# A delta-rule mixer on one core: the scales of the 16x16 solve by a transpose and one on-chip DMA, and the solve moved behind q's convolution

## The chip, the core and the metric

The kernel runs on one core of a Trainium2 chip. Times are microseconds of device time for one execution. The kernel before took 3308.4, 3311.98 and 3314.25 us in three timed runs; the middle one, 3311.98, is the time before. One more execution was profiled, and all rows are from that one. PE is TensorE, DVE is VectorE, ACT is ScalarE, POOL is GpSimd and SP is SyncE, which issues most of the DMAs.

## What is computed

The reference is one step of a decoder trunk of two layers for 1024 new prompt tokens and 64 sample tokens (8 sequences of 8). Layer 0 mixes tokens with a gated delta rule in 8 heads of 128 columns, layer 1 with HGRN2, and a convolutional feed-forward block follows each. The part that the change touches is the delta rule of one head, in chunks:

```
kb = kc * bc[..., None]
A = jnp.where(strict, jnp.einsum('nbhik,nbhjk->nbhij', kb, kc) * decay, 0.0)
rhs = jnp.concatenate([vc * bc[..., None], kb * jnp.exp(G)[..., None]], axis=-1)
sol = lax.linalg.triangular_solve(A + eye, rhs, left_side=True, lower=True, unit_diagonal=True)
def step(S, xs):
    u = uv_ - jnp.einsum('bhck,bhkv->bhcv', w_, S)
    o = jnp.einsum('bhck,bhkv->bhcv', qg_, S) + jnp.einsum('bhij,bhjv->bhiv', attn_, u)
    S = S * gl_[..., None, None] + jnp.einsum('bhck,bhcv->bhkv', kd_, u)
```

q, k and v come from a projection, a causal convolution of width 4 and a silu; q and k are normalised. The outputs of all heads go through a norm, a gate and the output projection.

## The kernel before

Dense fp32 products are made of three products in a shorter fp32 form: each operand is split into a high and a low part, and `dense` (L109 to L115) adds high by high, high by low and low by high. A weight tile is loaded by SP and split by ACT (L106) and DVE (L107). In the rows, `pp` are the projections of the heads, `po` and `pf` the output projection, and `adap` products of the conditioning that are spread over the heads; DVE adds those up in `adasb` (L184).

One head is a generator, `gdn_head(h)`. The main loop takes turns between two heads, so that the front of head h+1 (projections, decay, solve) stands beside the recurrence of head h. It resumes a generator at each `yield`. Within what the loop gives, the order of instructions on each engine is set by the framework's scheduler, from the program's order, its own cost model and the buffers that are free. Each engine runs its list in order: what stands behind a waiting instruction waits as well.

The steps of a head, in the order of the program: k is projected and convolved. The decay `dec` is made. `Z` is k by k times the decay (L794 to L804), stored to `zd` in DRAM. k is transposed, its norms give `rk`, and three DVE operations give `c1`, `nE` and `c2` (L826 to L828; in the rows these are `gc`). `nE` holds the scale of each token, 128 partitions by 9 columns. The solve wants it with one row of 16 tokens for each of 72 blocks (9 chunks of 8), which is the tile `Ep`, 72 by 16: POOL stores `nE` element by element to `ed` in DRAM (L829) and loads it back (L841). The diagonal blocks of Z come as `Zp` from `zd` (L838). Then q is projected and convolved, `pqk` (k by q, L846 to L855) is made, and q is transposed for its norm (`pq`).

Behind a yield stands the 16x16 solve: `Lp` is `Zp` times `Ep` (L868), and 15 steps of one product (L873) and one reduction (L875) on DVE invert the 72 lower triangles at once, followed by a copy (L876). All are in the tile `fs`. The inverse is stored to `td` (L878), loaded as `mg` (L879) so that four blocks of a chunk lie in their partitions, and ACT masks it (L889, L890). Then v and the gate g are projected. The merge follows: from 16x16 blocks to 32, 64 and 128, in products `pV` (L928, L952, L970), `pT` (L933, L958) and `pX` (L937, L961, L973) on PE, with DVE and ACT between. The first `pV` needs `mg`.

The recurrence goes over 8 chunks: `pKS` (k by S, L994), `ru` (DVE, L996), `pU` (L998), the copy `u` (ACT, L1000), `pS` (L1002), and the new state `sn` (DVE, L1011); `po` (L1005, L1006) collects the output. The sample tokens (L1019 on) and the norm and gate end the head; its output is transposed on PE (`pot`, L650), and POOL stores it to DRAM (`ohl`, L660 and L661). The output projection behind the last head loads these as `og` (L470).

PSUM tiles are of three kinds; transposes, `pqk`, merge products and the output `po` of a head share the three buffers of the kind `mx`.

Of the kernel before, what the change touches and what calls it, by code (L numbers as in the profile page):

```python
# [9 lines left out]
F32 = mybir.dt.float32  # L10
# [4 lines left out]
ALU = mybir.AluOpType  # L15
# [4 lines left out]
NT = 1024  # L20
NS = 64
NTOK = NT + NS
# [4 lines left out]
EPS = 1e-6  # L27
# [15 lines left out]
def trunk_kernel(ctx: ExitStack, tc: tile.TileContext, a: dict, o: dict):  # L43
    nc = tc.nc
# [4 lines left out]
    drp = ctx.enter_context(tc.tile_pool(name="drp", bufs=1, space=DRAM))  # L49

    def big(tag, shape=(128, NTOK), dt=F32, name=None, bufs=None):
        return main.tile(list(shape), dt, tag=tag, name=name or tag, bufs=bufs or {"xp": 2, "wraw": 3, "whl": 3}.get(tag, 1))

    def small(tag, shape, dt=F32, bufs=1, name=None):
        return sm.tile(list(shape), dt, tag=tag, name=name or tag, bufs=bufs)

    def ps(tag, name=None):
        return psp.tile([128, 512], F32, tag=tag, name=name or tag, bufs={"mm": 3, "mx": 3, "rc": 2}[tag])

    mm = nc.tensor.matmul  # L60


    def cload(name, shape, dt=F32):
        t = const.tile(list(shape), dt, name="c_" + name)
        nc.scalar.dma_start(out=t, in_=a[name])
        return t

    ident = cload("ident", [128, 128])
# [96 lines left out]
    def ada_row(l, i, k, tag, ptag, held):  # L165


        w = big(tag, [128, 1024], name="adaw")
        nc.sync.dma_start(out=w, in_=a["ada_w"][l, k * 128:(k + 1) * 128, i * 1024:(i + 1) * 1024])
        if held and k:  # L170
            pt = ada_acc[0]
        else:
            pt = ps(ptag, name="adap")
            ada_turn(None if held else pt)
        for q in range(4):
            mm(pt[32 * q:32 * q + 32, :256], cs[:, k, :], w[:, 256 * q:256 * q + 256], start=(not held or k == 0),
               stop=(not held or k == 7), tile_position=(0, 32 * q))
        if held:
            ada_acc[:] = [pt]
        if k == 0 and not held:  # L180
            ada_acc[:] = [small("adasb", [128, 256], bufs=1)]
            nc.scalar.activation(ada_acc[0], pt[:, :256], AF.Copy)
        elif not held:
            nc.vector.tensor_tensor(ada_acc[0], ada_acc[0], pt[:, :256], op=ALU.add)  # L184
        elif k == 7:
            ada_acc[:] = [small("adasb", [128, 256], bufs=1)]
            nc.scalar.activation(ada_acc[0], pt[:, :256], AF.Copy)
        if k == 7:
            ada_done.append((l, i, ada_acc.pop()))

    def ada_turn(pt=None):

        if not ada_done:
            return
        l, i, sb = ada_done.pop(0)
        p2 = (pt or ps("mx", name="adap2"))[:, 256:512]
        for j in range(2):
            nc.tensor.transpose(p2[:, 128 * j:128 * j + 128], sb[:, 128 * j:128 * j + 128], ident)
        nc.vector.tensor_tensor(
            mods[l][:, 8 * i:8 * i + 8, :].rearrange("p (q j) r -> p j q r", j=2),  # L200
            p2.rearrange("p (j q r) -> p j q r", q=4, r=32)[:, :, :, 0:9],
            adab[:, l, 8 * i:8 * i + 8].rearrange("p (q j) -> p j q", j=2).unsqueeze(3).to_broadcast([128, 2, 4, 9]), op=ALU.add)
# [198 lines left out]
    for g in GORD:  # L401
        hgs[g] = new_hg(g, f"h0{g}")
        t0, n = GRP[g][0], GP[g]
# [9 lines left out]
    for j in range(4):  # L413
# [6 lines left out]
        for g in GORD:  # L420
            t0, n = GRP[g][0], GP[g]
            sc, sh = mod(0, 1), mod(0, 0)
            pt = big("D10", [128, 2, 512], name="pnt")
            for m in range(2 * j, 2 * j + 2):
                t = pt[:, m % 2, :n]
                h = hgs[g][:, 0, m, :n]
# [317 lines left out]
    def ada_step():  # L744
        if rest:
            ada_row(*rest.pop(0), "D10", "mm", False)
        else:
            ada_turn()

    def gdn_head(h):  # L750
        par = h % 2
# [3 lines left out]
        def project(kind, dst):  # L755
            w = load_w(a["w_gin"][h, kind], 1024, "wi")
            return conv_silu(proj(w, hgs, "pp"), kind, h, dst)

        def transposes(src, name, each, evac):

            for b in range(3):
                p = ps("mx", name=name)
                for j in range(4 if b < 2 else 1):
                    t = 4 * b + j
                    n = 128 if t < 8 else 64
                    nc.tensor.transpose(p[:n, 128 * j:128 * j + 128], src[:, 128 * t:128 * t + n], ident)
                for j in range(4 if each and b < 2 else 1 if each else 0):
                    t = 4 * b + j
                    n = 128 if t < 8 else 64
                    each(p[:n, 128 * j:128 * j + 128], t, n)  # L770
                if evac:
                    evac(b, p)

        def sumsq(ss):
            def add(pj, t, n):
                jk = small("junk", [128, 128], bufs=1)
                nc.scalar.activation(jk[:n], pj, AF.Square, accum_out=ss[:n, t:t + 1])
            return add


        k = A(1, "k")
# [3 lines left out]
        dec = big("D2" if par else "D0", name="dec")  # L785
# [27 lines left out]
        def evac_k(b, p):  # L813
# [3 lines left out]
            else:  # L817
# [7 lines left out]
        c1, c2, nE = [small(f"gc{i}", [128, 9], bufs=2) for i in range(3)]  # L825
        nc.vector.scalar_tensor_tensor(c1, rk, 0.5, col(beta), op0=ALU.mult, op1=ALU.mult)  # L826
        nc.vector.scalar_tensor_tensor(nE, c1, -2.0, rk, op0=ALU.mult, op1=ALU.mult)
        nc.vector.tensor_tensor(c2, nE, col(eG), op=ALU.mult)  # L828
        nc.gpsimd.dma_start(out=ed[par].rearrange("(t k) i -> (k i) t", k=8), in_=nE)  # L829


        fs = big("D9", [128, 1024], name="fs")
# [4 lines left out]
        Ep = small("Ep", [72, 16])  # L837
        nc.gpsimd.dma_start(  # L838
            out=Zp, in_=zd[par].rearrange("t x -> (t x)").rearrange("(b y) -> b y", y=2064)[:, :2048].rearrange(
                "b (j i) -> b j i", i=128)[:, :, 0:16])  # L840
        nc.gpsimd.dma_start(out=Ep, in_=ed[par])  # L841
        yield

        q = A(0, "q")
        project(0, q)
        for b in range(3):  # L846
            pq = ps("mx", name="pqk")
            if b < 2:
                for j in range(4):
                    t0 = 512 * b + 128 * j  # L850
                    mm(pq[:, 128 * j:128 * j + 128], k[:, t0:t0 + 128], q[:, t0:t0 + 128], start=True, stop=True)
                nc.vector.tensor_tensor(dec[:, 512 * b:512 * b + 512], pq, dec[:, 512 * b:512 * b + 512], op=ALU.mult)
            else:
                mm(pq[:64, :64], k[:, NT:], q[:, NT:], start=True, stop=True)
                nc.vector.tensor_tensor(dec[:64, NT:], pq[:64, :64], dec[:64, NT:], op=ALU.mult)  # L855
        ada_step()
        qe = small("gqe", [128, 9], bufs=2)
        nc.vector.memset(qe[:, 8:9], 1.0)
        transposes(q, "pq", sumsq(qe), None)
        nc.vector.tensor_scalar(qe, qe, 128 * EPS, 512 * EPS * EPS, op0=ALU.mult, op1=ALU.add)  # L860
        eg = big("D0" if par else "D2", name="eg")
        nc.sync.dma_start(out=eg, in_=gd[1, h:h + 1, :].to_broadcast([128, NTOK]))
        nc.vector.tensor_tensor(q, q, eg, op=ALU.mult)
        qg = q

        yield

        tc.keep_in_program_order(nc.vector.tensor_tensor(Lp, Zp.rearrange("p j i -> p i j"), Ep.unsqueeze(2).to_broadcast([72, 16, 16]), op=ALU.mult))  # L868
        nc.gpsimd.memset(Tp, 0.0)
# [1 line left out]
        for i in range(1, 16):  # L871
# [8 lines left out]
                            in_=td[par].rearrange("(t k) (r x) -> (k r) t x", k=8, x=32))  # L880
# [7 lines left out]
        for e in range(2):  # L888
            nc.scalar.activation(XTc[:, :, :, e, :], cp[:, 0:8], AF.Copy, scale=m16e[:, e:e + 1])  # L889
            nc.scalar.activation(Xs[:, 16 * e:16 * e + 16], cp[:64, 8, 0, :], AF.Copy, scale=m16e[:64, e:e + 1])  # L890

        yield

# [147 lines left out]
        finish(0, h, ot, ot_s, so, qe, gnorm[:, 0:1], gt, ohl0, "D5")  # L1041

    heads = [gdn_head(h) for h in range(H)]

    def stage(h, n=1):
        for _ in range(n):
            if h < H:
                next(heads[h], None)
# [8 lines left out]
    for g in GORD:  # L1057
        p = ps("rc", name="pab")
        t0, n = GRP[g]
# [64 lines left out]
    for b in range(3):  # L1124
        pr = ps("mx", name="pgr")
        ts = [4 * b + j for j in range(4)] if b < 2 else [8]
        for j, t in enumerate(ts):
# [5 lines left out]
    gd = drp.tile([2, 8, NTOK], F32, name="gd")  # L1133
# [2 lines left out]


    zd = drp.tile([2, 9, 16512], F32, name="zd")
    ed = drp.tile([2, 72, 16], F32, name="ed")
    td = drp.tile([2, 72, 512], F32, name="td")  # L1140
    zero = big("D7", [128, 64], name="zero")
    nc.vector.memset(zero, 0.0)
# [1 line left out]
                        in_=zero[64:, :].unsqueeze(1).to_broadcast([64, 2, 64]))  # L1144
# [2 lines left out]
    ohl0 = [drp.tile([128, 2, NTOK], F32, name=f"ohl0{h}") for h in range(H)]  # L1147

    for h in range(H):
        stage(h, 3 if h else 4)  # L1150
        stage(h + 1)
        stage(h)
        stage(h + 1)
        stage(h, 2)
# [360 lines left out]
```

## Time and profile before

| what | value |
|---|---|
| median of three timed runs | 3311.98 us |
| profiled execution, its own time | 3303.52 us |
| its span | 3301.7 us |
| PE busy | 3172.5 us, 96% |
| DVE busy | 1672.8 us, 51% |
| ACT busy | 1101.9 us, 33% |
| POOL busy | 287.6 us, 9% |
| chain that ended last, by engine | PE 86%, DVE 7%, DMA 3%, ACT 2%, issue 2%, POOL 1% |
| the eight heads of layer 0 | about 60 to 840 us of the span |

Busy time is a sum over the whole span; in the heads' stretch the engines share the work differently from the feed-forward blocks. PEclk in a row of stretches is the granted clock of PE as a share of the full 2.4 GHz; 0.50 is the lower level, 1.2 GHz, and a value between is a mean over both. A wait is time in which an engine stood at the head of its list, put down to what released it last.

### The profile page before, as it was taken

How to read it: one execution, taken by the hardware profiler on the slowest of the kernel's cores; microseconds unless marked ns; L12 is line 12 of the kernel's file. 1: busy time of each engine (PE TensorE's matmuls, PEld its weight loads, DVE VectorE, ACT ScalarE, POOL GpSimd, SP SyncE). 2: the span in 40 equal slices, each digit the busy share in tenths (PEclk: the TensorE clock that was granted, in tenths of full speed). 3: DMA queues.
4: the chain of work that ended last, by engine and by line, in shares of the span. 5: the costliest groups of instructions: out<-in, count | busy, mean ns of one | idle time of the engine just before them, and what ended most of it. 6: DMA issues, size and time to landing. Idle time of an engine off the chain costs nothing.

```text
span 3301.7 us, 61857 instructions
## 1 busy us (share of the span) xinstructions
PE 3172.5 (96%) x25449; PEld 2948.0 (89%) x25449; DVE 1672.8 (51%) x3819; ACT 1101.9 (33%) x2611; POOL 287.6 (9%) x639
## 2 busy tenths in 40 slices
PE   7899999998999999999998999999998999999997
PEld 5888888887889999999996999999888999999997
DVE  6677777774562333333447645555465233333345
ACT  5344444442342313131234332333343331222222
POOL 0111111110100000000001000000010000000002
PEclk9999999998999999999998999999999999999999
DMA  6333333234312222222223111112531111111113
GB/s 205 96 105 99 100 100 99 77 93 151 118 61 87 84 83 86 84 87 81 92 63 113 57 62 59 60 63 83 189 104 46 46 46 46 44 44 46 41 63 106
DMA packets 164635, 277.98 MB, mean 84 GB/s; under 512 B 20056, under 2 KB 91480, under 8 KB 164352
## 3 DMA queue, kind: packets, MB, share of 16 engines
q1 hardware_dynamic: 145328, 236.24, 22.7%
q0 software_dynamic: 15616, 37.15, 3.8%
q8 instruction: 200, 3.28, 0.4%
q10 hardware_dynamic: 3408, 0.63, 0.1%
q14 instruction: 83, 0.68, 0.1%
HBM read 222.48 MB, written 51.47 MB: 83 GB/s over the span
## 4 chain that ended last, share of the span: by engine, by line
PE 86%; DVE 7%; DMA 3%; ACT 2%; issue 2%; POOL 1%; ACTq 0%; SPq 0%; POOLq 0%; DVEq 0%
PE pp L113 6%; PE pp L114 6%; PE pp L115 6%; PE pg L113 5%; PE pu L113 5%; PE pg L114 5%; PE pg L115 5%; PE pu L115 5%; PE pu L114 5%; PE pd L113 5%; PE pd L115 5%; PE pd L114 5%; PE pf L113 2%; PE pf L114 1%; PE pf L115 1%
## 5 line engine op out<-in xcount | busy, mean ns | idle before, releaser
L113 PE MATMUL pp<-h,wi 128*128 128x384 f32 (+1 forms) x1536 | 518.8, 339 | 11.9 <-DVE adasb L184 8.5
L115 PE MATMUL pp<-h,wi 128*128 128x384 f32 (+1 forms) x1536 | 518.3, 338 | 0.0
L114 PE MATMUL pp<-h,wi 128*128 128x384 f32 (+1 forms) x1536 | 515.8, 336 | 0.2 <-DVE h L305 0.2
L113 PE MATMUL pg<-h,wg 128*128 128x384 f32 (+1 forms) x1056 | 346.6, 329 | 0.0
L113 PE MATMUL pu<-h,wu 128*128 128x384 f32 (+1 forms) x1056 | 346.3, 328 | 0.0
L115 PE MATMUL pg<-h,wg 128*128 128x384 f32 (+1 forms) x1056 | 346.0, 328 | 0.0
L114 PE MATMUL pg<-h,wg 128*128 128x384 f32 (+1 forms) x1056 | 345.4, 327 | 0.4 <-DVE h L305 0.4
L115 PE MATMUL pu<-h,wu 128*128 128x384 f32 (+1 forms) x1056 | 344.8, 327 | 0.0
L114 PE MATMUL pu<-h,wu 128*128 128x384 f32 (+1 forms) x1056 | 344.3, 326 | 0.0
L113 PEld LDWEIGHTS pp<-h,wi 128*128 128x128 f32 x1536 | 292.4, 191 | 28.2 <-issue 9.0
L113 PE MATMUL pd<-mh,wd 128*128 128x384 f32 (+1 forms) x912 | 299.6, 330 | 0.0
L114 PEld LDWEIGHTS pp<-h,wi 128*128 128x128 f32 x1536 | 292.8, 191 | 6.0 <-DVE wi L107 1.2
L115 PEld LDWEIGHTS pp<-h,wi 128*128 128x128 f32 x1536 | 292.3, 190 | 6.6 <-issue 4.8
L115 PE MATMUL pd<-mh,wd 128*128 128x384 f32 (+1 forms) x912 | 297.4, 326 | 0.0
L114 PE MATMUL pd<-ml,wd 128*128 128x384 f32 (+1 forms) x912 | 297.1, 326 | 0.0
L113 PEld LDWEIGHTS pu<-h,wu 128*128 128x128 f32 x1056 | 198.2, 188 | 7.8 <-issue 6.2
L113 PEld LDWEIGHTS pg<-h,wg 128*128 128x128 f32 x1056 | 199.0, 189 | 6.8 <-issue 6.2
L114 PEld LDWEIGHTS pg<-h,wg 128*128 128x128 f32 x1056 | 199.0, 189 | 1.9 <-issue 1.2
L598 DVE TENSOR_TENSOR facc<-facc,pd 128x384 f32<-128x384 f32 (+1 forms) x192 | 97.6, 510 | 203.1 <-PE pd L115 203.1
L115 PEld LDWEIGHTS pg<-h,wg 128*128 128x128 f32 x1056 | 199.1, 189 | 0.0
L115 PEld LDWEIGHTS pu<-h,wu 128*128 128x128 f32 x1056 | 198.2, 188 | 0.0
L114 PEld LDWEIGHTS pu<-h,wu 128*128 128x128 f32 x1056 | 198.2, 188 | 0.0
(449 smaller groups left out, 5730.9 us busy)
## 6 DMA issues: line engine op xcount, KB each, us to landing
adaw<-in_ada_w SPq DMA_DIRECT2D x96, 512.0 KB, 3.8
wgr<-in_w_gu SPq DMA_DIRECT2D x88, 256.0 KB, 2.7
wur<-in_w_gu SPq DMA_DIRECT2D x88, 256.0 KB, 2.6
wir<-in_w_gin SPq DMA_DIRECT2D x64, 256.0 KB, 2.8
wdr<-in_w_dn SPq DMA_DIRECT2D x64, 256.0 KB, 2.6
wir<-in_w_hin SPq DMA_DIRECT2D x64, 256.0 KB, 2.7
og<-ohl SPq DMA_DIRECT2D x32, 384.0 KB, 7.5
xg<-xd SPq DMA_DIRECT2D x24, 384.0 KB, 4.8
```

The costliest lines, as they stand in the source:

```text
L113: mm(out, wh, rh(k), start=(first and i == 0), stop=False)
L114: mm(out, wh, rl(k), start=False, stop=False)
L115: mm(out, wl, rh(k), start=False, stop=(last and i == len(ks) - 1))
L598: nc.vector.tensor_tensor(am, am, p[:, :n], op=ALU.add)
```

## The change

The way of the scales is changed. PE transposes `nE` into a PSUM tile `pE` of 9 by 128 (kind `mx`), ACT copies it into a part of `fs` (`nEt`), and one DMA issued by SP carries it from there to `Ep`, on chip. The DRAM tile `ed` and the two POOL DMAs go.

The solve, its two DMAs and the two ACT masks move up: they stand directly behind q's projection and convolution, ahead of `pqk`, `pq` and the decay factor of q. One yield goes with that, and the main loop takes one step fewer in a head's first stage. The lines of the solve in the kernel after are L850 (`Lp`), L855, L857 and L858; the merge, recurrence and output lines are two more than before.

```diff
--- before.py
+++ after.py
@@ -826,7 +826,8 @@
         nc.vector.scalar_tensor_tensor(c1, rk, 0.5, col(beta), op0=ALU.mult, op1=ALU.mult)
         nc.vector.scalar_tensor_tensor(nE, c1, -2.0, rk, op0=ALU.mult, op1=ALU.mult)
         nc.vector.tensor_tensor(c2, nE, col(eG), op=ALU.mult)
-        nc.gpsimd.dma_start(out=ed[par].rearrange("(t k) i -> (k i) t", k=8), in_=nE)
+        pe = ps("mx", name="pE")
+        nc.tensor.transpose(pe[:9, :128], nE, ident)
 
 
         fs = big("D9", [128, 1024], name="fs")
@@ -838,11 +839,38 @@
         nc.gpsimd.dma_start(
             out=Zp, in_=zd[par].rearrange("t x -> (t x)").rearrange("(b y) -> b y", y=2064)[:, :2048].rearrange(
                 "b (j i) -> b j i", i=128)[:, :, 0:16])
-        nc.gpsimd.dma_start(out=Ep, in_=ed[par])
+        nEt = fs[:9, 256:384]
+        nc.scalar.copy(nEt, pe[:9, :128])
+        nc.sync.dma_start(out=Ep, in_=nEt)
         yield
 
         q = A(0, "q")
         project(0, q)
+
+        tc.keep_in_program_order(nc.vector.tensor_tensor(Lp, Zp.rearrange("p j i -> p i j"), Ep.unsqueeze(2).to_broadcast([72, 16, 16]), op=ALU.mult))
+        nc.gpsimd.memset(Tp, 0.0)
+        nc.gpsimd.memset(fs[:72, 512 + 16:1024:33], 1.0)
+        for i in range(1, 16):
+            pri = fs[:72, 0:i * i].rearrange("p (c j) -> p c j", j=i)
+            nc.vector.tensor_tensor(pri, Tp[:, 0:i, 0:i].rearrange("p j c -> p c j"),
+                                    Lp[:, i:i + 1, 0:i].to_broadcast([72, i, i]), op=ALU.mult)
+            nc.vector.tensor_reduce(Tp[:, i, 0:i], pri, axis=mybir.AxisListType.X, op=ALU.add)
+        nc.vector.tensor_copy(Xp, Tp.rearrange("p i c -> p c i"))
+        mg = big("D7", name="mg")
+        nc.gpsimd.dma_start(out=td[par], in_=fs[:72, 512:1024])
+        nc.gpsimd.dma_start(out=mg[:, 0:288].rearrange("p (t x) -> p t x", x=32),
+                            in_=td[par].rearrange("(t k) (r x) -> (k r) t x", k=8, x=32))
+
+        cp = mg[:, 0:288].rearrange("p (t i c) -> p t i c", i=2, c=16)
+        XTc = mg[:, 288:800].rearrange("p (t i e c) -> p t i e c", i=2, e=2, c=16)
+        Xs = mg[:64, 800:832]
+        x32 = mg[:, 288:800].rearrange("p (t i c) -> p t i c", i=2, c=32)
+        Xc, Tc = x32[:, :, 0, :], x32[:, :, 1, :]
+        EM, V = [mg[:, i:i + 256].rearrange("p (t c) -> p t c", c=32) for i in (0, 832)]
+        for e in range(2):
+            nc.scalar.activation(XTc[:, :, :, e, :], cp[:, 0:8], AF.Copy, scale=m16e[:, e:e + 1])
+            nc.scalar.activation(Xs[:, 16 * e:16 * e + 16], cp[:64, 8, 0, :], AF.Copy, scale=m16e[:64, e:e + 1])
+
         for b in range(3):
             pq = ps("mx", name="pqk")
             if b < 2:
@@ -862,32 +890,6 @@
         nc.sync.dma_start(out=eg, in_=gd[1, h:h + 1, :].to_broadcast([128, NTOK]))
         nc.vector.tensor_tensor(q, q, eg, op=ALU.mult)
         qg = q
-
-        yield
-
-        tc.keep_in_program_order(nc.vector.tensor_tensor(Lp, Zp.rearrange("p j i -> p i j"), Ep.unsqueeze(2).to_broadcast([72, 16, 16]), op=ALU.mult))
...
-            nc.scalar.activation(Xs[:, 16 * e:16 * e + 16], cp[:64, 8, 0, :], AF.Copy, scale=m16e[:64, e:e + 1])
 
         yield
 
@@ -1136,7 +1138,6 @@
 
 
     zd = drp.tile([2, 9, 16512], F32, name="zd")
-    ed = drp.tile([2, 72, 16], F32, name="ed")
     td = drp.tile([2, 72, 512], F32, name="td")
     zero = big("D7", [128, 64], name="zero")
     nc.vector.memset(zero, 0.0)
@@ -1147,7 +1148,7 @@
     ohl0 = [drp.tile([128, 2, NTOK], F32, name=f"ohl0{h}") for h in range(H)]
 
     for h in range(H):
-        stage(h, 3 if h else 4)
+        stage(h, 2 if h else 3)
         stage(h + 1)
         stage(h)
         stage(h + 1)
```

The order of the engines' lists moves in three places that matter below.

DVE, where the solve of head 4 begins. Before, it stands behind k by q of head 4 (`dec`, `q`) and beside v's convolution:

```order
L855 TENSOR_TENSOR dec<-pqk,dec 64x64
L732 SCALAR_TENSOR_TENSOR v<-gxp,c_gcw,v 128x1024
L863 TENSOR_TENSOR q<-q,eg 128x1088
L868 TENSOR_TENSOR fs<-fs,Ep 72x256
L739 SCALAR_TENSOR_TENSOR v<-gxp,v 128x1088
L860 TENSOR_SCALAR gqe<-gqe 128x9
L873 TENSOR_TENSOR fs<-fs 72x1
L107 TENSOR_TENSOR wi<-wir,wi 128x512
L875 TENSOR_REDUCE fs<-fs 72x1
```

After, it stands inside the recurrence of head 3, whose `ru` and `sn` are L998 and L1013:

```order
L1013 SCALAR_TENSOR_TENSOR sn<-sn,eGL,pS 128x128
L739 SCALAR_TENSOR_TENSOR q<-gxp,q 128x1088
L998 SCALAR_TENSOR_TENSOR ru<-pKS,gc_2907,vb 128x128
L850 TENSOR_TENSOR fs<-fs,Ep 72x256
L184 TENSOR_TENSOR adasb<-adasb,adap 128x256
L855 TENSOR_TENSOR fs<-fs 72x1
L107 TENSOR_TENSOR wi<-wir,wi 128x512
L1013 SCALAR_TENSOR_TENSOR sn<-sn,eGL,pS 128x128
L857 TENSOR_REDUCE fs<-fs 72x1
L855 TENSOR_TENSOR fs<-fs 72x4
L857 TENSOR_REDUCE fs<-fs 72x2
L855 TENSOR_TENSOR fs<-fs 72x9
```

The solve's first steps moved ahead of the end of head 3's recurrence, between the operations on which that recurrence's products wait.

PE, in the middle of head 3's recurrence. Before, one step reads:

```order
L998 MATMUL pU<-ru,X_911 128x128
L115 MATMUL pp<-h_266,wi 128x384
L113 MATMUL pp<-h_266,wi 128x384
L114 MATMUL pp<-h_266,wi 128x384
L1002 MATMUL pS<-ru,kd 128x128
L1006 MATMUL po_5014<-ru,dec 128x128
L115 MATMUL pp<-h_266,wi 128x384
L113 MATMUL pp<-h_266,wi 128x384
L994 MATMUL pKS<-sn,k 128x128
L1005 MATMUL po_5014<-sn,q 128x128
```

After, the step in which `pE` of head 4 comes:

```order
L114 MATMUL pp<-h_266,wi 128x384
L115 MATMUL pp<-h_266,wi 128x384
L830 MATMUL pE<-c_ident,gc_5006 9x128
L1008 MATMUL po_5023<-ru,dec 128x128
L1007 MATMUL po_5023<-sn,q 128x128
L1008 MATMUL po_5023<-ru,dec 128x128
L1007 MATMUL po_5023<-sn,q 128x128
L1004 MATMUL pS<-ru,kd 128x128
L1008 MATMUL po_5023<-ru,dec 128x128
L176 MATMUL adap<-adaw,cs 32x256
L996 MATMUL pKS<-sn,k 128x128
L1007 MATMUL po_5023<-sn,q 128x128
```

The transpose stands ahead of three steps' `po` products and of `pS` of its own step; the next step's `pKS` follows without a dense product between.

PE, around the first merge product `pV` of head 7, the last head. Before, it comes among the output projection's `po` products:

```order
L114 MATMUL po<-og_9114,wo 128x320
L115 MATMUL po<-og_9114,wo 128x320
L113 MATMUL po<-og_9114,wo 128x320
L928 MATMUL pV<-mg,Z 32x32 x32
L114 MATMUL po<-og_9114,wo 128x320
L115 MATMUL po<-og_9114,wo 128x320
L113 MATMUL po<-og_9114,wo 128x320
L114 MATMUL po<-og_9114,wo 128x320
L115 MATMUL po<-og_9114,wo 128x320
L933 MATMUL pT<-mg 32x32 x32
L937 MATMUL pX<-mg 32x32 x32
L952 MATMUL pV<-fs,Z 32x32 x16
```

After, it follows the last `pp` products directly, and `po` begins behind it:

```order
L115 MATMUL pp<-h_266,wi 128x384
L113 MATMUL pp<-h_266,wi 128x384
L114 MATMUL pp<-h_266,wi 128x384
L115 MATMUL pp<-h_266,wi 128x384
L930 MATMUL pV<-mg,Z 32x32 x32
L113 MATMUL po<-og_9127,wo 128x384
L114 MATMUL po<-og_9127,wo 128x384
L115 MATMUL po<-og_9127,wo 128x384
L113 MATMUL po<-og_9127,wo 128x384
L935 MATMUL pT<-mg 32x32 x32
L939 MATMUL pX<-mg 32x32 x32
L954 MATMUL pV<-fs,Z 32x32 x16
```

`pV`, `pT` and `pX` of the last head moved ahead of the first `po`. In the list before, 124 dense products stand between the `pot` of head 6 and this `pV`; in the list after, 28.

## Rows read from the trace of the kernel before

**Rows 1.** Stretches, one row each: length, busy per engine, PEclk, DMA share, GB/s.

```profile
206.00:292.00 86.00, 82.84 (x852) 72.43 (x850) 63.22 (x156) 38.34 (x127) 15.64 (x32) 1.00 0.38 102
```

**Rows 2.** Waits of PE, 140 to 740: total us, times, longest us.

```profile
PE pV L928 <- ACT mg L889: 13.7, 7, 2.9
PE pp L113 <- DVE adasb L184: 8.5, 1, 8.5
```

**Rows 3.** Chain of waits, 404 to 420: start us, us, what.

```profile
409.12 2.82 DMA td<-fs
...
416.69 0.75 PE pV L928 x50
```

**Rows 4.** Chain of waits, 140 to 166, head 0.

```profile
131.27 10.07 DMA ed<-gc
...
141.63 3.81 DMA Ep<-ed
...
156.53 2.24 DMA td<-fs
...
163.36 0.75 PE pV L928 x50
```

**Rows 5.** Waits of PE, 738 to 830, from head 7 on.

```profile
PE pV L928 <- ACT mg L889: 5.7, 1, 5.7
PE po L113 <- DMA og<-ohl: 3.6, 4, 2.1
```

**Rows 6.** Stretches of head 7, after the last projection.

```profile
740.00:758.00 18.00, 14.19 (x67) 12.17 (x67) 8.56 (x26) 2.36 (x5) 1.92 (x3) 0.91 1.03 356
758.00:764.00 6.00, 0.50 (x36) 0.50 (x40) 0.43 (x1) 1.66 (x5) 0.00 (x0) 0.85 0.61 207
764.00:782.00 18.00, 17.82 (x345) 15.71 (x336) 6.56 (x15) 5.33 (x14) 0.00 (x0) 0.86 0.10 31
782.00:790.00 8.00, 6.48 (x38) 4.43 (x40) 2.91 (x7) 2.84 (x11) 0.00 (x0) 0.79 0.11 35
790.00:800.00 10.00, 7.06 (x55) 4.95 (x56) 4.43 (x9) 2.45 (x8) 0.00 (x0) 0.99 0.18 59
800.00:812.00 12.00, 12.00 (x59) 9.12 (x59) 7.41 (x24) 3.72 (x17) 1.49 (x2) 0.58 0.49 154
```

**Rows 7.** Groups of PE, 140 to 830: transposes of a head's output.

```profile
L650 PE MATMUL pot<-c_ident,ot 128*128 128x128 f32 x64 | 8.6, 278 | 2.4 <-DVE ot L645 2.4
```

**Rows 8.** Groups of ACT, 140 to 830: copies of u.

```profile
L1000 ACT COPY ru<-pU 128x128 f32<-128x128 f32 x64 | 16.8, 263 | 68.5 <-PE pU L998 61.2 <-PE pp L115 4.0 <-issue 3.0
```

**Rows 9.** Stretches behind a wait for pV or for head 0's pp.

```profile
156.00:160.00 4.00, 3.49 (x11) 3.49 (x12) 3.96 (x6) 0.00 (x0) 2.04 (x3) 0.50 0.28 82
160.00:164.00 4.00, 3.00 (x74) 2.68 (x72) 1.20 (x2) 1.80 (x5) 0.41 (x2) 0.81 0.19 60
...
412.00:424.00 12.00, 10.24 (x265) 8.57 (x263) 7.10 (x12) 4.98 (x12) 2.06 (x4) 0.86 0.27 82
584.00:596.00 12.00, 10.03 (x266) 8.85 (x265) 7.02 (x13) 5.10 (x12) 2.06 (x4) 1.00 0.16 49
```

**Rows 10.** Groups of DVE, the solve: out<-in, xcount | busy us, mean ns | idle before.

```profile
L873 DVE TENSOR_TENSOR fs<-fs 72x1 f32<-72x1 f32 (+14 forms) x120 | 38.0, 317 | 2.4
...
L875 DVE TENSOR_REDUCE fs<-fs 72x1 f32<-72x1 f32 (+14 forms) x120 | 27.8, 232 | 2.6
```

**Rows 11.** Order of time, DVE, head 3's recurrence: start us, us, line, [idle before].

```profile
355.31 0.17 DVE L827 SCALAR_TENSOR_TENSOR gc<-gc,grk 128x9 f32<-128x9 f32 x1
...
365.59 0.35 DVE L996 SCALAR_TENSOR_TENSOR ru<-pKS,gc,vb 128x128 f32<-128x128 f32 x1 [1.70 <-PE pp L114]
...
372.61 0.35 DVE L996 SCALAR_TENSOR_TENSOR ru<-pKS,gc,vb 128x128 f32<-128x128 f32 x1 [0.58 <-PE pKS L994]
374.44 0.35 DVE L1011 SCALAR_TENSOR_TENSOR sn<-sn,eGL,pS 128x128 f32<-128x128 f32 x1 [1.48 <-PE pS L1002]
```

**Rows 12.** Order of time, POOL, 336 to 372, head 4.

```profile
366.22 0.58 POOL L841 DMA_DIRECT2D Ep<-ed  x1 [9.40 <-DMA ed<-gc]
```

More of the change, by code (lines that the diff above doesn't have):

```diff
@@ L845, in gdn_head @@
         project(0, q)
[L846 to L864, printed above, removed]
-        yield
         tc.keep_in_program_order(nc.vector.tensor_tensor(Lp, Zp.rearrange("p j i -> p i j"), Ep.unsqueeze(2).to_broadcast([72, 16, 16]), op=ALU.mult))
@@ L890, in gdn_head @@
             nc.scalar.activation(Xs[:, 16 * e:16 * e + 16], cp[:64, 8, 0, :], AF.Copy, scale=m16e[:64, e:e + 1])
+        for b in range(3):
+            pq = ps("mx", name="pqk")
+            if b < 2:
+                for j in range(4):
+                    t0 = 512 * b + 128 * j
+                    mm(pq[:, 128 * j:128 * j + 128], k[:, t0:t0 + 128], q[:, t0:t0 + 128], start=True, stop=True)
+                nc.vector.tensor_tensor(dec[:, 512 * b:512 * b + 512], pq, dec[:, 512 * b:512 * b + 512], op=ALU.mult)
+            else:
+                mm(pq[:64, :64], k[:, NT:], q[:, NT:], start=True, stop=True)
+                nc.vector.tensor_tensor(dec[:64, NT:], pq[:64, :64], dec[:64, NT:], op=ALU.mult)
+        ada_step()
+        qe = small("gqe", [128, 9], bufs=2)
+        nc.vector.memset(qe[:, 8:9], 1.0)
+        transposes(q, "pq", sumsq(qe), None)
+        nc.vector.tensor_scalar(qe, qe, 128 * EPS, 512 * EPS * EPS, op0=ALU.mult, op1=ALU.add)
+        eg = big("D0" if par else "D2", name="eg")
+        nc.sync.dma_start(out=eg, in_=gd[1, h:h + 1, :].to_broadcast([128, NTOK]))
+        nc.vector.tensor_tensor(q, q, eg, op=ALU.mult)
+        qg = q
         yield
```

## Prediction

> **What bounds the kernel now.** I first read the engines' busy time on the page: PE is busy 96% of the span, so the most that any change of order can win is PE's idle time and the time that it runs at the lower clock. The order of PE is the same in both kernels from the boundary behind head 7 on, so only the stretch of the eight GDN heads, about 60 to 840 us, can move. Second, the stretches by window: in the 86 us from 206 to 292, one head's period, PE is busy 82.84 us, so some 3 us of each head are idle [rows 1]. Third, PE's waits there: 13.7 us stand before `pV`, the first product of a head's merge, in seven waits of which the longest is 2.9, and 8.5 us stand before one `pp` product of head 0 [rows 2]. Fourth, the chain of waits around one such wait: the solve's result is stored to `td` at 409.12, loaded into `mg`, expanded by ACT, and `pV` starts at 416.69, so 7.6 us lie between the solve's end and `pV` with DMA in most of it [rows 3]. In head 0 the same chain begins earlier: the store of `ed` takes 10.07 us and its load back 3.81, then the solve, with `td` at 156.53 [rows 4]. The wait of 8.5 us is DVE's: `adasb` stands behind the solve in DVE's order, and the solve waits for `Ep`. Last, head 7 has no next head's projections beside it: `pV` waits 5.7 us and `po` 3.6 for `og` [rows 5], and from 740 to 812 the six stretches leave 3.81 + 5.50 + 0.18 + 1.52 + 2.94 + 0 = 13.95 us of PE idle [rows 6].
>
> **The change, part by part.** Durations are those of the profiled execution (3303.5 us, span 3301.7); the sum is made against it and carried to the median of 3312.0.
>
> *Head 0.* The new path is one transpose (278 ns by `pot`, which is larger [rows 7]), one ACT copy (263 ns by u [rows 8]) and one DMA. No row shows an on-chip DMA of this shape. From below I bound it by the `td` store, 2.82 us [rows 3], from above by the `ed` store, 10.07; nearest, in bytes and in 64-byte runs, is the load of `Ep`, 3.81 [rows 4], and I take that. So `Ep` is there about 4.4 us after the scales instead of 131.27 to 145.44, 14.2 us: the solve begins 9.8 us earlier and ends near 146.5. `adasb` then is done before PE needs it (its wait ended at 160 − 3.49 = 156.5 [rows 9], so it began at 148.0), and the 8.5 us go. With them goes the slow start behind: 156 to 160 ran at PEclk 0.50, the lower of the two levels, 1.2 GHz: half of 3.49 us, 1.75, is lost. `pV` comes next: its operands are ready 9.8 us earlier, 153.5, and PE, which stood 1.0 us in the stretch from 160 to 164 [rows 9], arrives 8.5 + 1.75 earlier than 162.4, at 152.1, so a wait of about 1.5 stays where 1.0 was. Head 0: 8.5 + 1.75 − 0.5, rounded down to 9; the upper bound of the DMA takes 6 of these back.
>
> *Heads 1 to 6, the wait of `pV`.* 13.7 less head 0's 1.0 is 12.7 us. By the new order the solve of head h stands in the recurrence of head h−1: in head 4 `Lp` comes behind the `ru` of 365.59 [rows 11]. With 8.2 us of its own on DVE and some 10 of other work between, it ends near 384, where the store was issued at 409.12 before: 25 us earlier, and 2.9 at most were missing. All 12.7 go. What is late next is the merge's own chain, which moves with `pV`. Behind `pV` three of four such stretches ran at PEclk 0.86 (412 to 424 is one, 498 to 510 and 668 to 680 read the same), the fourth at 1.00 [rows 9]: 10.24 x 0.14 = 1.4 us each, three of them, 4 us. I count it in, its bounds are 0 and 6.
>
> *Head 7's tail.* In the old order 124 dense products stand between `pot` of head 6 and `pV` of head 7, and `po`, which waits for `og`, is among what stands ahead of `pV`; in the new one 28, and `pV` stands ahead of the first `po`. The solve has ended before head 6's recurrence is over, so `td` and `mg` no longer meet the `og` loads, whose stretch had a DMA share of 1.03 [rows 6]. The 5.7 us of `pV` go, and the `po` products come between the steps of the recurrence that ran bare at 782 to 800 (1.52 + 2.94 idle). I leave 2 us of `og` waits and 1.5 of bare steps: 13.95 − 3.5 = 10.5. The clock: busy time by 1 − PEclk over the six stretches is 1.3 + 0.1 + 2.5 + 1.4 + 0.1 + 5.0 = 10.3 us [rows 6]; with PE full I leave 2.8. The tail gives 10.5 + 7.5 = 18, between 4 (the `pV` wait less a new wait for `og`) and 24 (all).
>
> *What it costs.* (a) `pE` is a wide fp32 product inside the F32R stream, and PE waits in order for nE, which comes off the end of a long row of small DVE operations: 0.28 + 0.2, say 0.5 per head, 8 x 0.5 = 4; between 2.2 (0.28 each) and 12 (with a wait of 1.2). `po` of three steps stands behind it, which nobody else waits for soon. ACT's copy stands ahead of u, which waits 0.3 longer. (b) The solve now lies on DVE between `sn` and `ru`, on which the recurrence's products wait. Its operations average 317 and 232 ns, 240 of them, 65.8 us, 8.2 per head [rows 10]. DVE is idle 0.58 us before `ru` and 1.48 before `sn` in such a step [rows 11]. Up to 7 operations, 1.2 us for the small ones, stand in one gap, so at most half a microsecond each in some steps is late, and PE has 2 to 6 dense products (about a microsecond) there. I take 0.5 per head, 7 heads, 3.5; bounds 0 and 31 (below). (c) DVE waits for `Ep` at `Lp`, with `sn` and `ru` queued behind it and PE behind those. nE is done at 355.5, the `ru` ahead of `Lp` ends at 365.9 [rows 11]: 10.4 us, against 4.4 needed. Cover of 6 us, so nothing. (d) POOL loses its issue of `Ep` and the 9.40 us wait ahead of it [rows 12]; POOL binds nothing here. SP gets one issue per head behind weight loads already issued.
>
> Sum: 9 + 12.7 + 4 + 18 − 4 − 3.5 = 36. Profiled 3267.5; the median of 3312 becomes 3276.
>
> **Rivals.** *The tail gives back nothing but its `pV` wait.* For it: the `og` loads keep the queue full, and the clock is 0.86 at 764 to 782 although PE is busy 17.82 of 18 there [rows 6], so a full engine alone does not bring it back; the merge's many small products and the switches between them and the dense ones stay. Then the tail is worth 4: 36 − 14 = 22, 3290. Against it: the bare steps at 782 to 800 are filled by the order itself. The Trainium skill (TensorE: Matmul & The Clock Gate, A second HAM failure mode: psum-queue depth-cycling) says that short idle gaps between groups of products can make the clock fall and rise by turns, which speaks against this change's clock terms, 7.5 and 4. The trace agrees at 764 to 782. By it alone the sum would be 36 − 11.5 = 24.5.
>
> *The solve delays the recurrence.* If none of the idle time on DVE took any of it, in a head the operations ahead of `sn` or `ru` (19 of them with `Lp` in head 4, at the reduce's mean of 0.232, 4.4 us [rows 10]) would all be PE's: 7 x 4.4 = 31, leaving 5: 3307. Against it: the two idle times, 2.06 us a step, are there [rows 11].
>
> *Slower: the new DMA is no faster than the old path.* The place is `Lp` on DVE in the recurrence of the head before. For it: no row shows a DMA from 9 partitions to 72, its runs are 64 bytes, it shares the queue of the weight loads, and the `ed` store of small pieces took 10.07 [rows 4]. The old path took 14.5 us in head 4 (355.5 to 366.22 [rows 12], and 3.81), which is 4.1 more than the 10.4 that are there. Then DVE, and PE with it, stand 4.1 us in seven recurrences, 29 us, and each such wait would cost a slow stretch like head 0's 1.75 us: 12. 36 − 41 = −5, and 2 us more in each makes it −19: 3317 to 3331. It decides from a landing about 13.8 us after nE (7 x (3.4 + 1.75) = 36). Against it: the load of `Ep`, also in 64-byte pieces, took 3.81. The Trainium skill (DMA: Bandwidth & Descriptors, Specifications) puts full rate at 512 bytes and more, and a read-modify-write below; so it speaks against the 64-byte runs too. The rows agree in direction, 10.07 for 4-byte pieces and 3.81 for 64-byte ones.
>
> **How the numbers follow.** My forecast 0.55 (its own range 3262 to 3286), the tail without its gain 0.17 (3290, 6 to either side), a larger gain, below 3260, 0.06; the solve's delay 0.10 (3307, of which 0.03 on the faster side), the slow DMA 0.12 (0.03 within and 0.09 above). A measurement tells some 0.2%, 6.6 us, from no change: 3305.4 to 3318.6. Faster 0.55 + 0.17 + 0.06 + 0.03 = 0.81; same 0.07 + 0.03 = 0.10; slower 0.09. The range leaves out most of the slow DMA and the upper half of the delay, and 0.03 below: 3258 to 3306.
>
> **What would show it.** Right: no wait of `pp` for `adasb` near 148; no wait of `pV` for ACT in heads 1 to 6 and under 2 in head 0; the on-chip DMA lands in 3 to 4.5 us, and DVE has no idle at `Lp`; head 7's `pot` comes some 40 us earlier than 812; the heads' period stays at or below 86 less 2 us. Wrong: a row of PE waits for `sn` or `ru` in the recurrences of several microseconds in total per head (the second rival), DVE idle at `Lp` with the DMA as its releaser (the third), `po` waits for `og` and PEclk below 0.9 between `pV` and `pot` of head 7 (the first).

## The result, and the profile after

The changed kernel takes 3273.38 us (median of four runs, 3271.93 to 3279.03) against 3311.39 for the kernel before in the same series (3308.4 to 3314.25): 38 us, a ratio of 0.990 with a 95% interval of 0.9888 to 0.9912. (The median before is of four runs here, the three of the section on the metric and one of 3310.79.) The forecast was 3276. The profiled span went from 3301.7 to 3270.2, 31.5 us; the execution profiled before was some 8 us under the median of its kernel, which is most of what the two differences differ by.

PE in the page of the kernel after (busy time, share of the span, instructions). It has the same work and eight transposes more, and 3156.9 instead of 3172.5 us busy: so part of the gain is that the same products take less time, and not only that PE waits less.

```profile
PE 3156.9 (97%) x25457; PEld 2940.0 (90%) x25457; DVE 1667.2 (51%) x3819; ACT 1099.0 (34%) x2619; POOL 275.9 (8%) x623
```

To see where the time went I cut both traces at two products that end the same work in both: the last projection `pp` of head 7 and the last `po` of the output projection's first half. Before, in order of time (start us, us, engine, line, out<-in):

```profile
739.12 0.34 PE L115 MATMUL pp<-h,wi 128*128 128x384 f32 x1
```

```profile
838.46 0.31 PE L115 MATMUL po<-og,wo 128*128 128x320 f32 x1
```

After:

```profile
728.32 0.34 PE L115 MATMUL pp<-h,wi 128*128 128x384 f32 x1
```

```profile
811.05 0.31 PE L115 MATMUL po<-og,wo 128*128 128x320 f32 x1
```

From the last `pp` to the last `po`, the tail of head 7, it is 99.3 us before and 82.7 after: 16.6. The heads come first: executions reach the first head up to 5 us apart, so they are counted from ACT's fourth split of a `wi` tile (90.0 and 89.4 us) to the last `pp`: 649.1 before, 638.9 after, 10.2. The rest of the span, behind the last `po`, is 2463.2 and 2459.1. The table has the same cuts for every run below; its first three columns are of one profiled execution each, its last is the median of the runs. The rest isn't in it: in the kernel after it was 2459.1, 2468.2 (e6) and 2467.5 (e1) in three executions of the same lists, so two executions can differ by 9 us for a reason that has nothing to do with the change.

| run | heads | tail | both | median us |
|---|---|---|---|---|
| before | 649.1 | 99.3 | 748.4 | 3311 |
| after | 638.9 | 82.7 | 721.6 | 3273.4 |
| after, again (e6) | 638.6 | 80.7 | 719.3 | 3273.5 |
| after, same lists (e1) | 643.5 | 75.4 | 718.9 | 3276.7 |
| last head late (e2) | 638.3 | 96.3 | 734.6 | 3296.1 |
| new scales only (e3) | 661.3 | 118.8 | 780.1 | 3331.6 |
| move only (e4) | 654.9 | 77.7 | 732.6 | 3299.0 |
| masks pinned (e5) | 631.3 | 76.9 | 708.2 | 3266.0 |
| two on-chip DMAs (e7) | 640.7 | 77.1 | 717.8 | 3273.8 |

PE's waits in the kernel after, 60 to 740 us (total, times, longest), the lines that answer to [rows 2] (which begins at 140; no wait of those two stands earlier):

```profile
PE pv L766 <- DVE v L739: 6.2, 5, 1.8
PE pV L930 <- ACT mg L871: 4.4, 1, 4.4
...
PE po L113 <- DMA og<-ohl: 2.6, 2, 2.3
...
PE pE L830 <- DVE gc L827: 0.5, 3, 0.2
```

The wait for `adasb` is gone, and of the seven waits of `pV` only head 0's is left, with 4.4 us instead of the 1.5 forecast. At the head of the list stands a wait that was 0.2 us before and isn't in the forecast: `pv`, the transposes of v, for DVE.

Stretches of the kernel after (length, then busy us of PE, its weight loads, DVE, ACT and POOL; granted clock, DMA share, GB/s). The first two answer to [rows 1], the others to [rows 6]:

```profile
206.00:292.00 86.00, 82.79 (x836) 72.61 (x835) 60.80 (x155) 37.14 (x121) 14.07 (x31) 1.00 0.32 100
292.00:378.00 86.00, 83.99 (x845) 73.55 (x845) 61.90 (x156) 37.00 (x120) 14.76 (x31) 1.00 0.35 108
728.00:734.00 6.00, 3.44 (x170) 2.57 (x168) 3.09 (x8) 1.01 (x2) 0.00 (x0) 1.00 1.04 391
734.00:752.00 18.00, 16.66 (x190) 14.98 (x182) 3.78 (x9) 3.72 (x9) 0.00 (x0) 0.62 0.80 283
752.00:775.00 23.00, 22.84 (x173) 18.18 (x171) 8.94 (x20) 8.70 (x34) 0.54 (x1) 1.00 0.16 50
775.00:788.00 13.00, 12.39 (x86) 11.54 (x86) 8.86 (x25) 4.74 (x12) 2.00 (x3) 1.00 0.43 142
788.00:811.00 23.00, 23.00 (x141) 23.00 (x140) 7.62 (x11) 11.05 (x27) 0.00 (x0) 1.00 0.68 223
```

The heads run at a granted clock of 1.00 in all six such stretches from 206 to 722 (0.98 in three of them before). The tail's first 24 us are still ragged: 2.56 us of PE idle in 728 to 734 with the DMA engines full, and then a clock of 0.62 for 18 us. From 752 on PE is all but full (58.23 of 59 us) at 1.00, where it had gaps and a lower clock before.

The new way of the scales in head 0, in order of time. On DVE (nE is L827, `Lp` L850):

```profile
126.27 0.17 DVE L827 SCALAR_TENSOR_TENSOR gc<-gc,grk 128x9 f32<-128x9 f32 x1
...
129.33 0.58 DVE L850 TENSOR_TENSOR fs<-fs,Ep 72x256 f32<-72x256 f32 x1
```

On SP:

```profile
127.09 1.01 SPq L844 DMA_DIRECT2D Ep<-fs  x1
```

`Lp` starts 2.9 us after nE ended, with no wait for `Ep`; so the transfer took at most 2.2 us from its issue. In no head does DVE wait for `Ep`; in heads 1 to 7 `Lp` stands 7.2 to 11.5 us behind nE.

### The profile page after: what moved, and what is told of

The parts are those of the page before. It is cut to its first block, busy times and chain, and to the rows that moved or that the text cites. A ratio compares the mean times of both kernels' runs of the same rounds, so it can differ in the third digit from the quotient of the medians.

```text
span 3270.2 us, 61821 instructions
## 1 busy us (share of the span) xinstructions
PE 3156.9 (97%) x25457; PEld 2940.0 (90%) x25457; DVE 1667.2 (51%) x3819; ACT 1099.0 (34%) x2619; POOL 275.9 (8%) x623
## 4 chain that ended last, share of the span: by engine, by line
PE 88%; DVE 5%; ACT 2%; DMA 2%; issue 2%; POOL 1%; ACTq 0%; SPq 0%; DVEq 0%; POOLq 0%
PE pp L114 7%; PE pp L113 7%; PE pp L115 6%; PE pu L113 5%; PE pg L113 5%; PE pg L114 5%; PE pg L115 5%; PE pu L115 5%; PE pu L114 5%; PE pd L113 5%; PE pd L115 5%; PE pd L114 5%; PE pf L113 1%; PE pf L114 1%; PE pf L115 1%
## 5 line engine op out<-in xcount | busy, mean ns | idle before, releaser
L113 PEld LDWEIGHTS pp<-h,wi 128*128 128x128 f32 x1536 | 291.5, 190 | 19.6 <-issue 11.3
```

The costliest lines, as they stand in the source:

```text
L113: mm(out, wh, rh(k), start=(first and i == 0), stop=False)
```

## The experiments

**e2: the last head's solve in its old place.** The rest is the changed kernel; the solve's code is in a function.

```diff
-        <solve, DMAs, masks>
+        if h < H - 1:
+            mg, cp, XTc, Xs, Xc, Tc, EM, V = solve()
 ...
         qg = q
+        if h == H - 1:
+            mg, cp, XTc, Xs, Xc, Tc, EM, V = solve()
```

> The changed kernel, but head 7 alone has its solve behind q's transposes and norm, the old place. Theory (what was won behind the last projection, 16.6 us from the last pp to the last po, comes from head 7's early solve alone, which lets pV stand ahead of the first po and po stand between the steps of the last recurrence): the stretch from last pp to last po is again 97 to 100 us, the pV wait 4 to 6 is back, time 3288 to 3292. Rival (a good part of the tail's gain is the clock that the heads before kept up, or the earlier start against the og loads): the stretch stays under 92 us, time under 3282.

Measured 3296.14 us (3291.19 to 3301.11), ratio to before 0.9955 (0.9941 to 0.997). PE's waits from 716 to 850:

```profile
PE pV L937 <- ACT mg L872: 7.0, 1, 7.0
PE po L113 <- DMA og<-ohl: 3.0, 1, 3.0
PE pS L1011 <- ACT ru L1009: 2.3, 6, 0.6
PE pU L1007 <- DVE ru L1005: 1.5, 4, 0.8
```

The tail is 96.3 us again, the `pV` wait is back with 7.0, and the steps of the recurrence, which has few dense products between them again, wait for ACT and DVE as before. The theory's numbers were a little off (97 to 100 for the tail, 4 to 6 for the wait, 3288 to 3292 for the time), but the rival's stretch under 92 us is excluded, and so the theory stands: the tail's gain is head 7's early solve and the order that follows from it. The two are not told apart. The heads keep their 638 us.

**e3: the new way of the scales alone,** in the kernel before.

```diff
-        nc.gpsimd.dma_start(out=ed[par].rearrange("(t k) i -> (k i) t", k=8), in_=nE)
+        pe = ps("mx", name="pE")
+        nc.tensor.transpose(pe[:9, :128], nE, ident)
 ...
-        nc.gpsimd.dma_start(out=Ep, in_=ed[par])
+        nEt = fs[:9, 256:384]
+        nc.scalar.copy(nEt, pe[:9, :128])
+        nc.sync.dma_start(out=Ep, in_=nEt)
```

> The kernel before with the new way of the scales alone (transpose, ACT copy, one on-chip DMA); the solve stays in its old place, and so do the yields. Theory (the new way shortens head 0 only, since in the other heads Ep was there long before the solve; the pV waits come from the solve's place): head 0's wait of pp for adasb, 8.5 us, goes, about 7 us; the pV waits of heads 1 to 6 stay at 10 to 15 us; time 3302 to 3307. The scheduler also leaves more bare steps in the last recurrence here, so up to 8 us worse is possible in the tail: to 3312. Rival (the new way carries most of the gain): 3285 or lower.

Measured 3331.62 us (3322.7 to 3342.02), ratio 1.0061 (1.0042 to 1.008): slower than before, outside both expectations. The wait for `adasb` did go, and PE still waits for `pV`:

```profile
PE pV L931 <- ACT mg L892: 16.3, 5, 5.0
```

But the scheduler's lists are others here. In PE's list 32 to 37 dense products now stand directly ahead of `pE` in the middle of the recurrences of heads 0 to 5 (5 to 9 in the changed kernel), and in the last head not one dense product stands between the merge's first product and the end of the recurrence. Stretches behind the wait of one head, and of the last recurrence:

```profile
500.00:510.00 10.00, 9.56 (x63) 8.64 (x61) 9.05 (x18) 2.81 (x6) 3.70 (x5) 1.00 0.39 128
510.00:520.00 10.00, 6.30 (x231) 5.60 (x232) 6.15 (x14) 4.08 (x11) 1.75 (x6) 0.58 0.14 42
520.00:530.00 10.00, 10.00 (x81) 8.55 (x81) 0.99 (x2) 2.25 (x5) 0.00 (x0) 0.50 0.01 2
530.00:540.00 10.00, 10.00 (x64) 8.05 (x64) 3.00 (x7) 3.73 (x18) 1.90 (x4) 0.73 0.17 48
780.00:800.00 20.00, 12.59 (x324) 11.24 (x322) 5.78 (x12) 5.10 (x13) 1.38 (x2) 0.70 0.20 56
800.00:820.00 20.00, 17.71 (x83) 12.70 (x82) 5.05 (x12) 4.49 (x16) 0.00 (x0) 0.53 0.05 14
```

The tail is 118.8 us. In the heads the stretch from 510 shows a second loss: 510 to 520 has 3.70 us of PE idle and a clock of 0.58, the next 10 us are at 0.50 with PE busy 10.00 of 10, and the next at 0.73. What the new way would be worth in lists that are otherwise those of before is left open; no such run was made.

**e4: the move alone,** with the scales through DRAM as before (the reverse of the edit above, in the changed kernel).

> The changed kernel with the old way of the scales through DRAM (store of ed, load of Ep, both on POOL); the solve has its new place. In DVE's order Lp then comes one to two steps of the recurrence later than in the changed kernel. Theory (the old way takes 14.5 us after nE, 10 of it in the store; Lp one or two steps later has 13 to 16 us): head 0 keeps its 8.5 us wait, heads 1 to 7 wait 0 to 3 us each at Lp with PE behind; the pV waits of heads 1 to 6 stay away; time 3280 to 3295. Rival (the way of the scales is hidden in every head but 0): 3280 at most, no DVE wait for Ep in heads 1 to 7.

Measured 3298.98 us (3291.35 to 3307.6), ratio 0.9968 (0.9956 to 0.998). DVE at the `Lp` of head 1 (in brackets the idle time before it and its releaser), and PE's waits:

```profile
207.23 0.58 DVE L847 TENSOR_TENSOR fs<-fs,Ep 72x256 f32<-72x256 f32 x1 [8.12 <-DMA Ep<-ed]
```

```profile
PE pKS L993 <- DVE sn L1010: 11.0, 4, 7.2
PE pp L113 <- DVE adasb L184: 8.8, 1, 8.8
```

DVE stands 8.12 us for `Ep` in head 0's recurrence and 1.72 and 1.58 in two later ones, and PE behind it at `pKS`, 11.0 us in four waits; head 0 keeps its 8.8. In the other heads `Lp` stands late enough in DVE's list. The time is above the 3280 to 3295 expected, and the wait of 8.12 above the 0 to 3. The heads take 16 us more than in the changed kernel, the tail is not longer. By the medians the old way costs some 25 us once the solve stands early, lists and all; this is the mechanism that the forecast had as its slower rival, and the new way escapes it by being five times as quick (2.9 us after nE in head 0, for 14.6 before). The rival of this experiment, that the way is hidden in every head but 0, falls.

**e7: the on-chip DMA twice,** one behind the other.

```diff
+        Eq = small("Eq", [72, 16])
-        nc.sync.dma_start(out=Ep, in_=nEt)
+        nc.sync.dma_start(out=Eq, in_=nEt)
+        nc.sync.dma_start(out=Ep, in_=Eq)
```

> The changed kernel with the on-chip DMA of the scales made twice, one behind the other (nEt to a second tile, that to Ep). Theory (one takes about 2.2 us from issue to landing, and Lp comes 9.6 us after nE in heads 1 to 7, so some 6 us of cover are left): DVE never waits for Ep in heads 1 to 7, the heads' period stays, time within 5 us of the changed kernel's, what differs comes from head 0, whose solve starts 2 us later. Rival (the DMA's landing is what the recurrence waits for, in pieces too small to see): 7 x 2 = 14 us slower.

Measured 3273.82 us (3271.09 to 3278.84), the changed kernel beside it on the same chip 3273.45 (e6). DVE never waits for `Ep`, with the second DMA issued 2.0 to 3.2 us after the first, whose landing it needs. So that much of the cover that the forecast worked out is there, and the rival's 14 us are not.

**e1 and e5: the new wait.** In order of time in head 4 of the kernel after (idle before in brackets):

```profile
383.34 0.51 ACT L871 ACTIVATE mg<-mg,c_m16e 128x256 f32<-128x256 f32 x1 [2.72 <-DMA mg<-td]
...
386.80 1.10 ACT L738 ACTIVATE gxp<-v 128x1088 f32<-128x1088 f32 x1
...
387.94 1.29 DVE L739 SCALAR_TENSOR_TENSOR v<-gxp,v 128x1088 f32<-128x1088 f32 x1 [1.50 <-ACT gxp L738]
...
389.29 0.98 PE L766 MATMUL pv<-c_ident,v 128*128 128x128 f32 x7 [0.98 <-DVE v L739]
```

ACT stands 2.72 us at the first mask of `mg` for its load; v's tanh (L738) is behind the masks and q's squares in ACT's list, v's last convolution step waits 1.50 for it on DVE, and PE's `pv` 0.98 for that. In all heads ACT waits at the masks (total, times, longest; before, then after):

```profile
ACT mg L889 <- DMA mg<-td: 37.2, 8, 15.1
```

```profile
ACT mg L871 <- DMA mg<-td: 26.6, 8, 6.8
```

So ACT's wait for the load is not new, it was longer before; what is new is that v's tanh stands behind it.

e1 moves the masks down in the program:

```diff
-        <masks, behind the solve's DMAs>
 ...
         qg = q
+        <masks>
```

> The changed kernel with one edit: ACT's four masks of mg stand behind q's transposes and norm in the program, where they stood before, while the solve and its two DMAs keep their new early place. Theory A (ACT is in order, the masks wait 26.6 us in eight pieces for the load of mg, and v's tanh, v's last convolution step on DVE and the pv transposes on PE are queued behind them): PE's wait of pv for v, 6.2 us in five pieces, falls under 1.5, ACT's wait for mg falls under 8, and the time comes 4 us lower, 3269. Rival B (the solve's 8 us of DVE work per head push the output scaling and v's convolution later): the pv waits stay near 6 and the time near 3273.

The scheduler's lists came out word for word those of the changed kernel, so e1 tells nothing between the theories; it is a second measurement of the changed kernel: 3276.7 us (3269.36 to 3278.81). e5 pins the place:

```diff
+        tanh[0] = nc.scalar.activation(xp, dst, AF.Tanh, scale=0.5)
 ...
         project(2, v)
+        with tc.issue_after(tanh[0].ins):
+            <masks>
```

> The changed kernel with ACT's four masks of mg issued behind v's tanh (an order pinned in the program); PE's, POOL's and SP's lists stay word for word those of the changed kernel, DVE's differ by the place of one EM product per head. The run before this with the masks moved in the program only left every list as it was, so it was a second look at the changed kernel. Theory A (ACT waits at the masks for the load of mg, 26.6 us in eight pieces, and v's tanh stands behind): ACT's wait for mg under 8 us, PE's wait of pv for v from 6.2 to under 2, time 4 us under the changed kernel's in the same call. Rival B (the solve's 8 us of DVE work per head make v late): pv waits stay at 5 to 7 us, time the same.

> The changed kernel once more, beside the others on one chip: 3268 to 3280, the pv wait 5 to 7 us, ACT's wait for mg 25 to 30.

e5 measured 3266.01 us (3263.3 to 3266.73), ratio to before 0.9862 (0.9847 to 0.9877); the changed kernel beside it on the same chip (e6) 3273.45 (3269.0 to 3281.99). PE's and ACT's waits in e5:

```profile
PE pV L933 <- ACT mg L899: 4.4, 1, 4.4
PE pot L650 <- DVE ot L645: 3.1, 7, 0.6
```

```profile
ACT mg L899 <- DMA mg<-td: 11.3, 3, 6.8
```

And PE's in the changed kernel beside it (e6):

```profile
PE pv L766 <- DVE v L739: 5.5, 5, 1.5
PE pV L930 <- ACT mg L871: 4.5, 1, 4.5
```

The `pv` waits are gone altogether, PE's list being the same; the solve's DVE work was not their cause. By the medians 7.4 us come back, against 4 expected, and the ranges of the four runs each do not meet; e5 beats both kernels, 45.6 us under the one before. ACT's wait at the masks fell to 11.3 us and not under 8. DVE's list differs by the place of one product per head; what that did is not told apart.

## Why the forecast was right, point by point

*The total.* 36 us forecast, 38 by the medians. Heads forecast 18.2 (9 + 12.7 + 4 − 7.5), measured 10.2, 10.5 and 5.6; tail forecast 18, measured 16.6, 18.6 and 23.9, each in three executions of the same lists. Heads and tail together gave 27 to 30 of the 36. That the medians show 38 is luck, and not owed to a step of the forecast: the sum was made on an execution that was 8 us quicker than the median, and where the slower ones lose their time no trace shows.

*Head 0.* Forecast 9; ACT's 13th split of a `wi` tile came 94.9 us behind the fourth before and 88.3 after, so 6.6. The transfer was better than taken (2.2 us for 3.8), the 8.5 us wait went. But `pV` waits 4.4 us, not 1.5: the chain of waits behind head 0's solve has

```profile
145.94 4.44 DMA td<-fs
...
150.66 3.04 DMA mg<-td
...
154.87 1.08 PE pV L930 x64
```

where the store of `td` takes 4.44 us against 2.24 [rows 4]. In the other heads of the changed kernel it lands 3.8 to 5.9 us after its issue, against 2.82 in [rows 3], so head 0 is no exception; there the early solve covers it. What makes it slower stays open.

*Heads 1 to 6.* The 12.7 us of `pV` are gone and the clock is 1.00, both as forecast, but the heads behind head 0 gained 3.6 us (10.2 less 6.6), where 9.2 were forecast. The step that failed is the sentence "What is late next is the merge's own chain". Late next was ACT: the masks moved up with the solve, ahead of q's squares and v's tanh, and ACT works in order. The forecast counted ACT's copy of the scales and never the four masks, which wait for a DMA. The price by the medians is 7.4 us (e5 against e6), and with the masks pinned the heads gain 17.8 against the forecast 18.2.

*The costs.* (a) The transposes wait 0.5 us in all for nE, and eight at 0.27 to 0.28, as the 0.278 of [rows 7], take 2.2, so 2.7 for 4. (b) The solve in the recurrence, 3.5 forecast: PE's list of waits of the kernel after has none for `sn` or `ru` in the heads, so nothing that shows. (c) The cover of `Ep` held (e7). These costs were put too high by some 5 us, which made up for part of what the masks took.

*The tail.* Right in place and size (e2). Its parts in the first profile: PE's idle time in the tail went from some 14 us to 4.7, about as forecast. The clock gave back less than the 7.5 that were forecast: it stood at 0.62 for 18 us, and 16.66 x 0.38 = 6.3 of the 10.3 are lost as before, so 4.0 came back. Some 3 us of the 16.6 I can't place. The 24 us behind the last `pp` in three executions of the same lists (after, e6, e1):

```profile
728.30:752.30 24.00, 20.10 (x350) 17.56 (x349) 6.81 (x16) 4.73 (x11) 0.00 (x0) 0.72 0.85 306
```

```profile
731.30:755.30 24.00, 19.97 (x366) 16.93 (x365) 7.65 (x18) 6.01 (x14) 0.00 (x0) 0.79 0.87 314
```

```profile
734.10:758.10 24.00, 21.52 (x394) 18.08 (x393) 8.88 (x21) 7.03 (x17) 0.00 (x0) 1.00 0.82 284
```

The longest wait of PE for `og` there was 2.3, 3.0 and 1.0 us, and only the third kept its clock at 1.00. So what is left of the tail's loss may hang on the `og` loads; that is not shown, and loading them earlier was not tried.

*The rivals.* The slow DMA did not come; e4 shows its mechanism at work. The tail without its gain did not come, though part of its clock loss did. What this rival read from 764 to 782, that a full PE alone does not bring the clock back, is the mean of two parts of the kernel before: with PE full, 764 to 769 ran at 0.50 and 769 to 782 at 1.00, so it came back within the stretch. The solve's delay came neither in the recurrence nor through DVE. Its sum, 36 − 31 = 5, takes the 3.5 of (b) twice; with them put back it is 8.5, some 3303 instead of 3307.

*The signs.* The waits for `adasb`, for `pV` in heads 1 to 6 and for `Ep` were absent as said. `pV` of head 0 waited 4.4 us for under 2, and the DMA landed sooner than the 3 to 4.5. Head 7's `pot` came at 780.9 instead of 812.4, 31.5 us earlier and not 40. The period of a head, between the last projections of heads 1 and 7, fell from 85.2 to 84.2 us (83.2 in e5), half of the 2 us named.

## What to carry to other kernels

A step that is moved takes everything that it issues with it: list each engine's instructions of the step and ask of each what it waits for in its new place and what is queued behind it; here four small masks on ACT cost 7.4 us beside a gain of 38, and pinning them behind v's tanh gave it back. Where a scheduler makes the lists, the parts of a change do not add up: the two parts alone gave +21 and −12 us, together −38, so read the lists of each variant before its time.

## What the runs showed of the hardware

- The granted clock can stay down while PE is full: in e3, a stretch with 3.70 us of idle was followed by 10 us at 0.50 with PE busy 10.00 of 10. The Trainium skill (TensorE: Matmul & The Clock Gate, A second HAM failure mode: psum-queue depth-cycling) says that frequent brief idle gaps between groups of products make the clock go up and down; the tail before, with 0.91, 0.85, 0.86, 0.79, 0.99 and 0.58 in turn [rows 6], agrees. The same lists gave 0.72, 0.79 and 1.00 in the same 24 us of three executions.
- Executions of one kernel differ with their granted clock, though not only with it. Of 15 runs of the kernel before, the three with a mean clock of 0.980 or more took 3302.6 to 3306.6 us, the other twelve 3308.3 to 3316.6; the profiled one had 0.981. Four runs of the changed kernel (e6) took 3269.0, 3272.3, 3274.6 and 3282.0 us at mean clocks of 0.988, 0.983, 0.983 and 0.979. In e1, with the same lists, the slowest, 3278.8, had 0.985 and one of 3277.8 had 0.981.
- A DMA on chip from 9 partitions to 72, in 64-byte runs, took 2.2 us at most in head 0; in e7, where a second one needs the first, the two were issued 2.0 to 3.2 us apart. The store of the same 4.5 KB to DRAM in 4-byte pieces took 10.07 and its load 3.81 [rows 4].
